# A hybrid diffusion layer on one core: modulation rows built by GpSimd inside the attention, block sums divided between the last head group and VectorE

## The chip, the core and the metric

The kernel runs on one NeuronCore of a Trainium2 chip. The metric is the device time of one execution in microseconds (us). Three runs of the kernel before took 1834.32, 1835.56 and 1839.87 us; their median is 1835.56.

Engine names: PE is TensorE (PEld its weight loads), DVE is VectorE, ACT is ScalarE, POOL is GpSimd, SP is the engine whose queue issues most DMAs.

## What is computed

One layer over 1024 latent tokens and 256 context tokens, width 1024, in float32. Cut to what matters here:

```python
mod = silu(c) @ w_mod + b_mod                  # 6 parts of 1024
sh1, sc1, g1, sh2, sc2, g2 = split(mod, 6)
hx = rmsnorm(x, norm1_g) * (1 + sc1) + sh1
q, k, v, u, B, C, ga, gc = split(hx @ w_in)    # context: k, v alone
o = windowed_attention(rope(q), rope(k), v, k_ctx, v_ctx, sink)
y = B * conv3(C * u)                           # depthwise, width 3
merged = sigmoid(ga) * (o @ w_pa) + sigmoid(gc) * (y @ w_pc)
x = x + g1 * (merged @ w_out)
hx2 = rmsnorm(x, norm2_g) * (1 + sc2) + sh2
x = x + g2 * expert_choice_moe(hx2)            # 16 experts, 128 tokens each
return rmsnorm(x, final_norm_g)
```

The modulation parts sh1 and sc1 are needed at the start. The four parts g1, sh2, sc2 and g2 (parts 2 to 5, called rows here) are needed only after the products of this document: g1, sh2 and sc2 in the output projection, g2 in the experts.

## The kernel before

Float32 products are made from two fp32r parts: a high part (a copy on ScalarE) and a low part (a subtraction on VectorE or GpSimd), and three products of them.

The stages, in order: the first modulation parts and the projection to q, k and v (0 to 240 us); the attention; the products for the convolution and the branch projections; the output projection with the router; the experts (from some 1230 us).

**Attention** (`Unit`, L571 to L651, and the loop from L693). There are 32 units, 4 groups of 4 heads by 8 blocks of 128 queries. While unit n is turned and multiplied with the values, the scores of unit n+2 are computed: PE (L605, L606), a reduction on VectorE (L608), the exponential on ScalarE (L613), then `normalise` (L617): small VectorE steps on 128x4 (L620, L622, L623) and four multiplications of the probabilities by GpSimd (L625). The transposes of a unit (L630, into two PSUM tiles named psT) need these. Between them a filler (`pour`) puts in the products of the gate blocks (L40 to L44), whose weights pass through three SBUF tiles named raw. In units 4, 10, 16 and 22 `x_sums` (L653) makes the block sums of x by ten GpSimd steps of 128x512 (L657); it uses two raw tiles. No order is written out for this part: a planner orders each engine's instructions by readiness and by their place in the program, and tile reuse gives the waits.

**Product stage** (`Pair`, the loop from L1056). From here the order of all five engines is the written one. Twenty pairs of 128-column blocks are multiplied by a scheme of seven block products (`product`, L850, 12 matmuls each on L795) instead of eight: sums of weights by VectorE (`sums13`, L826; `sums24`, L837), splits of these (`split_big`, `split22`, `split11`, ScalarE on L809 and VectorE on L810), partial sums from PSUM (L1088, L1121) and the four results (`quad`, L856). Pairs 0 to 11 give C, U and B blocks in turn (kinds 0, 1, 2), where a B pair also does the convolution (`conv`, L899) on ScalarE and VectorE (L907 to L910); pairs 12 to 15 multiply the attention output, 16 to 19 y. Their right-hand operands are block sums too: of the attention output (`o_rows`, `sums_of`, `sums_out`, L927 to L942, four sets by at_turn on L1008) and of y (four sets, L994). `op_load` and `op_split` (L950, L967) bring them in during pairs 11 and 15 and split them. `at_turn(n, slot, f)` hangs a step behind product slot `slot` of pair n.

**Rows** (`Row`, L732 to L766; L998 to L1006). In the same stage the four rows are made, one in each three pairs: eight DMAs of 128x1024 of w_mod by SP, each scaled by silu(c) on ScalarE (L743) and added up by GpSimd (L745); then a split (L751, L752), a DMA of the bias issued by GpSimd (L754), and in pairs 2, 5, 8 and 12 `total`: four matmuls with a column of ones (L760) into psT or psa tiles, two VectorE additions of the bias (L761, 1x512 each), for sc2 one more step with norm2_g (L765), and a DMA to DRAM (`rowd`). The matmuls stand ahead of slot 6:

```python
            if n in (2, 5, 8, 12) and slot == 6:
                st["row"].total([psT(), psT()] if n % 2 == 0 else [psa.tile([128, 512], F32, name=f"w{c}") for c in range(2)])
```

An odd pair takes its results in `psT(), psT(), psB(), psF()` (L848), an even one in four psa tiles; so a row's tiles are those that the pair after it takes first.

## Time and profile before

| | |
|---|---|
| median of 3 runs | 1835.56 us |
| profiled execution, its own time | 1834.67 us |
| span of its instructions | 1832.9 us |
| granted clock, mean over the span | 0.967 of full speed |
| attention, first transpose to the last | 256.3 to 583.6 us |
| gate products alone | 583.6 to 614.6 us |
| product stage | 614.6 to 1086.9 us |

The span runs from the first to the last instruction; 1.8 us lie around it. Busy time of an engine is the sum of its instructions; a row of windows gives, for a stretch, the busy time of each engine, how many instructions it ran, and the granted clock of PE as a share of 2.4 GHz. Matmuls overlap their neighbours, so their own durations are longer than their distance.

### The profile page before, as it was taken

Reading aid. Unit: us, or ns where it says so; the run is one execution under the profiler, and the core shown is the slowest. Engines: PE = TensorE matmul, PEld = TensorE weight load, DVE = VectorE, ACT = ScalarE, POOL = GpSimd, SP = SyncE. Lnnn points to the kernel's source line nnn. Section 1 sums busy time; section 2 is a strip of 40 time slices with the busy share of each in tenths; the row PEclk is TensorE's granted clock in tenths of the full one; section 3 lists DMA queues with packets and bytes.
Section 4 is the critical chain, followed back from the end, with each engine's and each line's share of the span. In section 5 each row is a group of like instructions: output and inputs, shape, how many; then the busy total and the mean of one; then the engine's idle time right before and its main releaser. Section 6 shows DMA issues by size and latency. Waiting matters only on the chain.

```text
span 1832.9 us, 24346 instructions
## 1 busy us (share of the span) xinstructions
PE 1717.3 (94%) x8421; PEld 1386.4 (76%) x8421; DVE 1462.0 (80%) x1990; ACT 1041.4 (57%) x1482; POOL 574.7 (31%) x372
## 2 busy tenths in 40 slices
PE   8999999999999989888799889959999999999997
PEld 5778878888888867667577667847888888888875
DVE  6756558788775488887987885578999999999997
ACT  5643167677775334333444343226777887877875
POOL 0000326355231145365763322241023223322101
PEclk8999999999999989898899999978999999999999
DMA  9353354243423737346657245678999999999955
GB/s 342 130 161 115 127 183 141 80 152 123 146 62 107 264 102 228 123 133 229 231 161 253 71 137 200 242 283 325 338 398 396 385 398 395 385 398 396 343 196 195
DMA packets 210861, 415.71 MB, mean 227 GB/s; under 512 B 17643, under 2 KB 107051, under 8 KB 209202
## 3 DMA queue, kind: packets, MB, share of 16 engines
q1 hardware_dynamic: 182226, 368.20, 56.1%
q0 software_dynamic: 6912, 25.51, 4.7%
q10 hardware_dynamic: 21600, 20.45, 3.2%
q8 instruction: 66, 1.08, 0.2%
q14 instruction: 57, 0.47, 0.1%
HBM read 343.31 MB, written 70.80 MB: 226 GB/s over the span
## 4 chain that ended last, share of the span: by engine, by line
PE 65%; DVE 13%; issue 4%; ACT 2%; DMA 1%; POOL 1%; POOLq 0%; ACTq 0%; DVEq 0%; SPq 0%
PE psA L1639 19%; PE w L795 5%; PE psB L1639 5%; PE psF L1639 5%; PE psA L1223 4%; PE psT L630 3%; PE psT L795 3%; PE psF L40 2%; PE psF L42 2%; PE psF L44 2%; PE psB L643 2%; PE psB L642 2%; PE psA L605 2%; PE psA L606 2%; PE psT L1624 2%
## 5 line engine op out<-in xcount | busy, mean ns | idle before, releaser
L1639 PE MATMUL psA<-part,xeh 128*128 128x512 f32 x1024 | 281.9, 392 | 0.5 <-ACT xeh L1627 0.5
L1639 PEld LDWEIGHTS psA<-part,xeh 128*128 128x128 f32 x1024 | 191.4, 188 | 40.0 <-ACT xeh L1627 1.0
L1674 POOL DMA_INDIRECT md<-ye,idxs x15 | 109.0, 7265 | 213.1 <-DVE ye L1671 213.1
L1639 PE MATMUL psA<-part,xel 128*128 128x512 f32 x512 | 163.5, 390 | 0.0
L625 POOL TENSOR_SCALAR p<-p,l 128x640 f32<-128x640 f32 (+1 forms) x128 | 100.1, 801 | 177.3 <-DVE l L623 52.6
L1497 DVE TENSOR_TENSOR part<-er,part 128x1024 fp32r<-128x1024 f32 x118 | 138.4, 1219 | 5.4 <-ACT part L1495 2.0
L1495 ACT CAST part<-er 128x1024 fp32r<-128x1024 f32 x118 | 123.7, 1057 | 32.9 <-PE psA L1639 19.9
L809 ACT CAST whi<-raw 128x1024 fp32r<-128x1024 f32 x40 | 42.0, 1050 | 172.2 <-DVE raw L840 111.0
L608 DVE CUSTOM_DVE_ANT_0 sn<-psA,msk,nsink 128x640 f32<-128x640 f32 (+1 forms) x128 | 107.4, 844 | 23.9 <-PE psA L606 13.8
L634 DVE TENSOR_TENSOR tl<-psT,th 128x512 fp32r<-128x512 f32 x152 | 104.0, 687 | 26.3 <-ACT th L633 24.9
L745 POOL TENSOR_TENSOR mp<-mp,mp 128x1024 f32<-128x1024 f32 x28 | 73.7, 2632 | 151.2 <-ACT mp L743 150.2
L633 ACT CAST th<-psT 128x512 fp32r<-128x512 f32 x152 | 88.4, 585 | 50.2 <-PE psT L630 49.3
L613 ACT ACTIVATE p<-sn,nm 128x640 f32<-128x640 f32 (+1 forms) x128 | 102.9, 805 | 21.7 <-DVE nm L608 19.6
L1639 PEld LDWEIGHTS psA<-part,xel 128*128 128x128 f32 x512 | 96.3, 188 | 20.5 <-DVE xel L1628 0.3
L1497 DVE TENSOR_TENSOR part<-mh,part 128x1024 fp32r<-128x1024 f32 x88 | 105.1, 1220 | 5.1 <-ACT part L1495 2.4
L1497 DVE TENSOR_TENSOR part<-ml,part 128x1024 fp32r<-128x1024 f32 x88 | 105.3, 1219 | 4.3 <-ACT part L1495 1.6
L1495 ACT CAST part<-ml 128x1024 fp32r<-128x1024 f32 x88 | 92.2, 1052 | 26.0 <-PE psA L1639 17.5
L1495 ACT CAST part<-mh 128x1024 fp32r<-128x1024 f32 x88 | 92.1, 1052 | 25.2 <-PE psA L1639 16.6
L1497 DVE TENSOR_TENSOR part<-mp,part 128x1024 fp32r<-128x1024 f32 x85 | 100.8, 1219 | 6.7 <-ACT part L1495 3.8
L1495 ACT CAST part<-mp 128x1024 fp32r<-128x1024 f32 x88 | 91.9, 1052 | 24.7 <-PE psA L1639 16.2
L1639 PE MATMUL psB<-part,hhh 128*128 128x512 f32 x256 | 98.6, 396 | 0.2 <-ACT hhh L1627 0.2
L810 DVE TENSOR_TENSOR wlo<-raw,whi 128x1024 fp32r<-128x1024 f32 x40 | 52.9, 1322 | 55.5 <-ACT whi L809 55.5
(506 smaller groups left out, 4730.9 us busy)
## 6 DMA issues: line engine op xcount, KB each, us to landing
raw<-in_w_in_dram SPq DMA_DIRECT2D x49, 512.0 KB, 5.6
er<-in_w_exp_down_dram SPq DMA_DIRECT2D x47, 512.0 KB, 8.8
er<-in_w_exp_up_dram SPq DMA_DIRECT2D x38, 512.0 KB, 5.6
mp<-in_w_exp_gate_dram SPq DMA_DIRECT2D x36, 512.0 KB, 6.0
mh<-in_w_exp_up_dram SPq DMA_DIRECT2D x33, 512.0 KB, 5.8
ml<-in_w_exp_up_dram SPq DMA_DIRECT2D x33, 512.0 KB, 6.2
mp<-in_w_mod_dram SPq DMA_DIRECT2D x32, 512.0 KB, 5.4
er<-in_w_exp_gate_dram SPq DMA_DIRECT2D x32, 512.0 KB, 5.5
```

What stands on the lines that cost most here:

```text
L608: nc.vector.tensor_tensor_reduce(out=sn, in0=sp[:, 512 - n:768], in1=msk.rearrange("p a b -> p (a b)")[:, mo * 128:mo * 128 + n + L], op0= ...
L613: nc.scalar.activation(out=p, in_=sn, func=AF.Exp, scale=-1.0, bias=self.nm4[:, h:h + 1], accum_out=self.l4[:, h:h + 1])
L625: nc.gpsimd.tensor_scalar(self.pr[h], self.pr[h], l4[:, h:h + 1], 1.0, op0=OP.mult, op1=OP.mult)
L633: nc.scalar.copy(out=th, in_=pt)
L634: nc.vector.tensor_tensor(out=tl, in0=pt, in1=th.bitcast(F32), op=OP.subtract)
L745: nc.gpsimd.tensor_tensor(out=self.acc, in0=self.w[k], in1=self.acc, op=OP.add)
L795: nc.tensor.matmul(ps_, lhsT=w[a][:, o + k], rhs=xs[b][:, k], start=(first and k + a + b == 0), stop=(k == 3 and a == 1), skip_group_check ...
L1223: nc.tensor.matmul(pa[:, s], lhsT=a[t // 2][k // 4][:, k % 4, ts], rhs=w[k][:, s], start=(j == 0 and a is mh and w is woh), stop=(j == NK ...
L1495: nc.scalar.copy(out=hi, in_=raw)
L1497: eng.tensor_tensor(out=lo, in0=raw, in1=hi.bitcast(F32), op=OP.subtract)
L1639: nc.tensor.matmul(outs[s], lhsT=lh[:, k], rhs=wt[:, s * 512:s * 512 + 512], start=(k == 0 and n == 0), stop=(k == NK - 1 and n == 2))
L1674: nc.gpsimd.indirect_dma_start(out=md, out_offset=bass.IndirectOffsetOnAxis(ap=idxs[:, e:e + 1], axis=0), in_=ye, in_offset=None, compute_ ...
```

## The change

Rows. The class `Row` and all its calls in the product stage are removed. `mod_row`, a generator, makes a row during the attention: w_mod is loaded into raw tiles, scaled and added by GpSimd alone, split by ScalarE and GpSimd, summed over partitions by four matmuls whose left operand is a two-column one-hot, so that the two halves of the row land in two partitions of one psT tile, and completed by VectorE on 2x512. One step of it is called in slots 1 and 4 of every unit except 4, 10, 16 and 22; a row has ten steps. Its two accumulators lie in a new pool `os`, closed at the end of the attention; the pool `tmp` of the product stage takes its place.

Block sums of the attention output: sets 0 and 1 (heads of groups 0 and 2) are made by GpSimd in units 25 to 31, in the tiles of `os`; sets 2 and 3 stay in pairs 2 and 5 and are subtracted by VectorE. Block sums of y: all four sets are subtracted by VectorE in place of GpSimd. `sums_of`, `sums_out` and `o_rows` move up in the file and take the engine or the tiles as arguments.

```diff
+    onehot = consts.tile([128, 4], FR, name="onehot")
...
+        for i in range(3):
+            nc.vector.tensor_scalar(onehot[:, i:i + 1], ones, float(i == 1), None, op0=OP.mult)
...
+    def sums_of(eng, which, ks, p11, p12, p21, p22):
+
+        for o_, a, b in ((p11, p12, p11), (p12, p22, p12), (p22, p22, p11), (p21, p21, p22)):
+            eng.tensor_tensor(out=o_, in0=a, in1=b, op=OP.subtract)
...
+    def mod_row(n):
+
+        part = n + 2
+        acc = osp.tile([128, 1024], F32, name=("o1", "o2")[n % 2])
+
+        def load(k):
+            w = raw_tile()
+            nc.sync.dma_start(out=w, in_=w_mod[k * 128:(k + 1) * 128, part * 1024:part * 1024 + 1024])
+            return w
+
+        w = load(0)
+        yield
+        for k in range(NK):
+            nc.gpsimd.tensor_scalar(w if k else acc, w, sf[:, 0, k:k + 1], 1.0, op0=OP.mult, op1=OP.mult)
+            if k:
+                nc.gpsimd.tensor_tensor(out=acc, in0=w, in1=acc, op=OP.add)
+            if k < NK - 1:
+                w = load(k + 1)
+                yield
+        small = raw_tile()
+        br, nr = small[0:2, 0:512], small[0:2, 512:1024]
+        nc.sync.dma_start(out=br, in_=b_mod[:, part * 1024:part * 1024 + 1024].rearrange("o (h f) -> (o h) f", h=2))
+        if part == 4:
+            nc.sync.dma_start(out=nr, in_=norm2_g.rearrange("o (h f) -> (o h) f", h=2))
+        hi = stage.tile([128, 1024], FR, name="raw", bufs=3)
+        lo = osp.tile([128, 1024], FR, name=("o1", "o2")[1 - n % 2])
+        nc.scalar.copy(out=hi, in_=acc)
+        nc.gpsimd.tensor_tensor(out=lo, in0=acc, in1=hi.bitcast(F32), op=OP.subtract)
+        yield
+        pf = psT()[0:2]
+        for hf in range(2):
+            cs = slice(hf * 512, hf * 512 + 512)
+            for v in (hi, lo):
+                nc.tensor.matmul(pf, lhsT=onehot[:, 1 - hf:3 - hf], rhs=v[:, cs], start=(hf == 0 and v is hi), stop=(hf == 1 and v is lo))
+        nc.vector.tensor_tensor(out=br, in0=pf, in1=br, op=OP.add)
+        if part == 4:
+            nc.vector.scalar_tensor_tensor(out=br, in0=br, scalar=1.0, in1=nr, op0=OP.add, op1=OP.mult)
+        yield
+        nc.sync.dma_start(out=rowd[n].rearrange("(h f) -> h f", h=2), in_=br)
...
+        if n in (25, 29):
+
+            o1, o2 = (osp.tile([128, 2, 512], F32, name=f"o{a}") for a in (1, 2))
+            o = o_rows((n - 25) // 4, o1.rearrange("p a b -> p (a b)"), [o2[:, 0], o2[:, 1]])
+        if n in (27, 31):
+            sums_of(nc.gpsimd, *o)
+            sums_out(*o)
...
+            if s in (1, 4) and n not in (4, 10, 16, 22):
+                next(mod_steps, None)
...
     for m in range(4):
-        at_turn(3 * m + 4, 2, lambda: sums_of(*st["ys"]))
+        at_turn(3 * m + 4, 2, lambda: sums_of(nc.vector, *st["ys"]))
...
-    for ks, b in enumerate((17, 38, 59, 68)):
-        at_turn(0, b - 5, lambda ks=ks: o_rows(ks))
-        at_turn(0, b, lambda: sums_of(*st["o"]))
+    for ks, b in ((2, 17), (3, 38)):
+        at_turn(0, b - 5, lambda ks=ks: o_late(ks))
+        at_turn(0, b, lambda: sums_of(nc.vector, *st["o"]))
...
-            if n in (2, 5, 8, 12) and slot == 6:
-                st["row"].total([psT(), psT()] if n % 2 == 0 else [psa.tile([128, 512], F32, name=f"w{c}") for c in range(2)])
```

## Rows read from the trace of the kernel before

**Rows 1.** The page, part 1: busy time of each engine over the span.

```profile
PE 1717.3 (94%) x8421; PEld 1386.4 (76%) x8421; DVE 1462.0 (80%) x1990; ACT 1041.4 (57%) x1482; POOL 574.7 (31%) x372
```

**Rows 2.** Windows by stage: from:to, length, busy of each engine, PEclk, DMA share, GB/s.

```profile
256.30:514.90 258.60, 255.72 (x1486) 217.17 (x1487) 206.47 (x436) 189.28 (x400) 120.12 (x133) 1.00 0.41 124
...
614.60:847.80 233.20, 206.52 (x853) 163.48 (x852) 182.29 (x166) 86.06 (x99) 102.83 (x48) 0.93 0.50 161
847.80:935.10 87.30, 68.09 (x257) 51.06 (x255) 77.11 (x54) 39.22 (x42) 67.05 (x29) 0.90 0.57 193
```

**Rows 3.** Windows by pair: pairs 1, 2, 3, 5, 8, 9, 10, 12 and 16.

```profile
634.00:653.40 19.40, 19.40 (x86) 15.79 (x85) 14.38 (x14) 9.52 (x11) 8.59 (x4) 1.00 0.64 192
653.40:682.70 29.30, 20.72 (x90) 15.71 (x88) 26.06 (x22) 8.72 (x10) 14.92 (x8) 0.92 0.18 53
682.70:704.70 22.00, 22.00 (x84) 17.71 (x85) 15.37 (x19) 7.99 (x9) 4.06 (x2) 0.88 0.69 221
...
724.20:754.50 30.30, 21.00 (x90) 15.76 (x88) 27.00 (x22) 8.82 (x10) 18.16 (x9) 0.92 0.31 96
...
795.80:825.60 29.80, 21.01 (x89) 15.74 (x87) 26.50 (x22) 8.82 (x10) 17.56 (x9) 0.93 0.29 93
825.60:847.80 22.20, 22.20 (x84) 17.86 (x85) 14.02 (x18) 7.99 (x9) 1.57 (x1) 0.87 0.74 260
847.80:873.50 25.70, 21.52 (x86) 16.79 (x85) 21.41 (x17) 9.40 (x11) 25.07 (x13) 0.93 0.63 200
...
893.70:935.10 41.40, 26.96 (x89) 18.59 (x87) 37.82 (x25) 18.34 (x20) 28.06 (x11) 0.84 0.39 134
...
994.20:1029.00 34.80, 25.34 (x85) 18.36 (x84) 31.42 (x22) 16.16 (x20) 23.05 (x9) 0.80 0.37 126
```

**Rows 4.** Waits from 614.6 to 847.8 us: us in total, times, longest us.

```profile
PEld psT L795 <- DVE mp L761: 14.7, 2, 7.4
...
PEld w L795 <- DVE mp L761: 7.3, 1, 7.3
```

**Rows 5.** Windows around the end of pair 2.

```profile
675.40:682.70 7.30, 0.37 (x3) 0.01 (x1) 7.26 (x6) 0.00 (x0) 5.34 (x3) 0.67 0.00 0
682.70:686.70 4.00, 4.00 (x9) 3.13 (x10) 2.78 (x4) 1.99 (x2) 0.00 (x0) 0.50 0.57 206
```

**Rows 6.** Two lines of VectorE: duration in ns, min/median/max, first and last start.

```profile
L829 DVE TENSOR_TENSOR raw<-raw x20: 675/682/2301, 595.8 to 1060.7; 128x512 f32<-128x512 f32 x20
...
L875 DVE TENSOR_TENSOR q<-w,q x16: 676/683/685, 688.0 to 1072.7; 128x512 f32<-128x512 f32 x16
```

**Rows 7.** Timeline of GpSimd and VectorE in pair 11: start us, us.

```profile
891.73 10.22 POOL L974 TENSOR_TENSOR t<-t,t 128x2048 fp32r<-128x2048 f32 x2 [3.30 <-ACT t L973]
...
889.44 1.27 DVE L908 SCALAR_TENSOR_TENSOR mp<-mp,cols,mp 128x1023 f32<-128x1023 f32 x1
...
891.95 5.58 DVE L908 SCALAR_TENSOR_TENSOR mp<-mp,cols,mp 128x1023 f32<-128x1023 f32 x1
```

**Rows 8.** Groups by shape, 614.6 to 847.8 us: busy us, mean ns.

```profile
L745 POOL TENSOR_TENSOR mp<-mp,mp 128x1024 f32<-128x1024 f32 x22 | 56.9, 2585 | 150.9 <-ACT mp L743 150.2
L930 POOL TENSOR_TENSOR mp<-mp 128x512 f32<-128x512 f32 x7 | 11.0, 1565 | 0.2
...
L810 DVE TENSOR_TENSOR x<-raw,x 128x1024 fp32r<-128x1024 f32 x9 | 11.0, 1217 | 0.0
```

**Rows 9.** GpSimd and VectorE steps of the attention: two of a timeline, three by line.

```profile
302.00 3.14 POOL L625 TENSOR_SCALAR p<-p,l 128x640 f32<-128x640 f32 x4
...
314.67 2.71 POOL L625 TENSOR_SCALAR p<-p,l 128x512 f32<-128x512 f32 x4
...
L625 POOL TENSOR_SCALAR p<-p,l x128: 689/803/1782, 255.6 to 570.7; 128x640 f32<-128x640 f32 x96, 128x512 f32<-128x512 f32 x32
...
L657 POOL TENSOR_TENSOR raw<-x,x x16: 1279/1294/2277, 178.6 to 446.0; 128x512 f32<-128x512 f32 x16
...
L620 DVE TENSOR_TENSOR es<-sink,nm x32: 150/161/1184, 252.6 to 567.6; 128x4 f32<-128x4 f32 x32
```

70 lines of the change are left out of this document (17 added, 53 removed).

## The prediction, made before the change was run

> **What bounds the kernel now.** I read the busy shares first: PE is busy 94% of the span and POOL 31% [rows 1], so a gain has to come from the places where PE stands still, and GpSimd has room somewhere. The windows by stage show where [rows 2]. In the attention (256.3 to 514.9 us) PE is busy 255.7 of 258.6 us and POOL 120.1. In pairs 0 to 9 of the product stage PE is busy 206.5 of 233.2 us, at a granted clock of 0.93, in pairs 10 to 12 only 68.1 of 87.3, while DVE is busy 182.3 and 77.1 us.
>
> The windows by pair [rows 3] give the unit of the argument. An undisturbed pair (pair 1; 0, 4, 7, 14, 15 and 17 to 19 are within 0.3 us of it) takes 19.4 us, all of it PE. Over that, pairs 2, 5 and 8 take 9.9, 10.9 and 10.4 us more and pair 3 2.6 more (6 the same) and pair 9 2.8: 39.2 us together. Pair 10 is 6.3 over, pair 12 22.0, pair 16 15.4; pairs 11 and 13 are 0.8 and 0.9 over. So 85 us of the stage are not products. The waits name the first cause [rows 4]: PE waited three times, 22 us, for VectorE's additions on L761, the last step of a modulation row, which hold a PSUM tile that the next pair wants first. The windows around the first of them show what follows [rows 5]: PE did 0.37 us of work in 7.3 us, and the next 4 us ran at a granted clock of 0.50, the lower level (1.2 GHz). That is the excess of pairs 3, 6 and 9.
>
> Why VectorE is so late there is seen in the price of one instruction [rows 6]: L829, with both inputs in SBUF, takes 0.68 us at the median and 2.30 at worst, while L875 with one input in PSUM stays between 676 and 685 ns. In the timeline [rows 7] a conv step on VectorE takes 1.27 us while GpSimd is quiet and 5.58 us beside a 128x2048 subtraction of GpSimd. So each two-input instruction of GpSimd is paid on VectorE too, when VectorE reads two SBUF operands. The Trainium skill ("SBUF — State Buffer", section "SBUF: two separate sides") calls the port pair of the two an exclusive lock, held for a whole instruction; the trace agrees in kind. By that rule each of the two such subtractions of pair 12 could hold VectorE for its whole 5.1 us and (c) below would be nearer to its lower bound; by the row one costs 4.3 us, and the sum goes by the row.
>
> **The change, part by part.**
> (a) Row work out of pairs 0 to 9. GpSimd loses 22 additions of 2.59 us there (56.9 us), 3 row splits of the same size and all 20 block-sum subtractions (such as L930's seven of 1.57 us) [rows 8]; nothing else of GpSimd's busy 102.8 us is left [rows 2]. ScalarE loses its multiplications by L743, PE the 12 row matmuls, SP its row loads, VectorE the six L761 additions. VectorE gains subtractions at the free price: 8 for two sets of block sums of y and 8 for two of the attention output, 16 x 0.68 = 10.9 us. Is VectorE fast enough then? Per pair it has seven 512-wide steps (two sums before, two after, one split, two partial sums) at 0.68 and three 1024-wide splits at 1.22 [rows 8], so 8.4 us; a finished C block costs 3 more steps, a U or B block 7 each (11.6 us per three pairs), the convolution four at 1.27, the moved sums 2.7 per set. Three pairs: 25.2 + 11.6 + 5.1 + 5.4 = 47.3 us against 58.2 us of PE. Only pairs 2 and 5 are over, 8.4 + 4.8 + 5.1 + 2.7 = 21.0 against 19.4; the 1.6 us run into a pair with 13 us of work. I leave 3 us of the 39.2 and take a gain of 36. Bounds: 25 (only the three waits of 7.3 us and the 12 matmuls go, VectorE stays late) and 39.
> (b) Pair 10. GpSimd was busy 25.1 of its 25.7 us, all of it row additions and block sums, all gone. VectorE gets one y set (2.7) in a pair that then needs about 16. Taken: 5.5 of 6.3; bounds 0 and 6.3.
> (c) Pair 12. The two 128x2048 subtractions of the operand split stay on GpSimd, and with them VectorE's two slow conv steps [rows 7]. What goes: one row addition in the queue ahead of them (2.6), the row split between them and the next operand split (2.6), the bias row's DMA (0.5 of GpSimd's time) and the last four row matmuls (0.9): 6.6, and VectorE enters the pair less late. Taken 8 of 22; bounds 0 and 18. The y sums of pair 13, now on VectorE, wait there for the late multiplications and the DMA that stores y; behind them stand a split and two sums that PE needs half a pair later, so I cost them at nothing; without that cover they cost their 2.7.
> (d) Pair 16: two operand splits collide with no row near. No change.
> (e) What the attention pays. Sixteen row matmuls come in; at 19.4/84 = 0.23 us each 3.7 us, and PE has no idle time to put them in. Four times one of two transpose tiles is held for a VectorE addition; I add 2.3 for that. ScalarE's four copies and SP's 32 loads lie beside it, as do the one-hot's three tiny steps. The GpSimd work must fit: a 128x640 multiplication is 0.785 and a 128x512 one 0.68 [rows 9], so 128x1024 is 0.785 + 3 x 0.107 = 1.11 (estimate); an addition is 2.59. Per row 8 x 1.11 + 8 x 2.59 = 29.6, four rows 118.4; with the 120.1 of before 238.5 of 258.6 us: 92% busy. Per unit it is 2 x 3.7 + 3.1 for the softmax scaling (L625), 10.5 against a unit of 258.6/25 = 10.3; it fits only because four units carry none, and because this stretch isn't held to the written order: the first block sums of x, written in unit 4, ran at 178.6 us [rows 9], so steps can move ahead to where GpSimd idles. VectorE's softmax steps on L620 have two SBUF inputs and can be blocked (161 ns at the median, 1184 at worst); VectorE has 52 us free in this stretch. SP's loads rotate over three shared raw tiles; a late addition holds a load, and the queries of the next unit stand behind it. Taken: 6 us; bounds 3.7 (nothing is removed here, so no gain) and 40.
> The two attention-output sums on GpSimd in the last group (8 x 1.29 = 10.3 us) stand where no row steps are left: nothing. Their tiles must be free before the first product's copy at about 617 us, 30 us after the last unit: nothing.
>
> Sum: 36 + 5.5 + 8 - 6 = 43.5 us. The profiled execution took 1834.67 us, 0.9 below the median of the runs; 1834.7 - 43.5 = 1791.2, against the median 1792. About 0.3% (5.5 us) is what a measurement of this kernel can tell from no change.
>
> **Rivals.**
> R1, GpSimd saturates. If VectorE's blocks stretch its work by the fifth that L930 shows (1.57 against 1.29 us [rows 8, 9]), 238.5 becomes 286, 28 us over the stretch: the attention pays 28 instead of 6, and the time is 1834.7 - 49.5 + 28 = 1813. For: 92% is close to full. Against: L657 keeps 1294 ns at the median in this very stretch, where VectorE mostly reads PSUM. The Trainium skill ("GPSIMD Engine Reference", section "4.1 Engine selection") speaks for this one: it sends elementwise work on a tile to VectorE, since two-input work is about twice as slow on GpSimd. The rows agree (1294 against 682 ns).
> R2, slower than before. GpSimd runs its queue in order; if row steps stand ahead of each unit's scaling, the transposes behind it become the bound of every unit. At 1.11 + 2.59 twice and the scaling at up to 1.78 each (its worst), a unit would take 14.5 us. It decides from 12.3 us per unit on, where 25 units give back 50. At 12.6 the attention pays 58: 1834.7 - 49.5 + 58 = 1843. Against: PE stood still for only 2.9 us of this stretch [rows 2], with three of the four block sums of x (ten steps of 1.29 us each) already in the same queue.
> R3, VectorE stays the bound. The added subtractions land in the conv pairs, the waits of L761 go but the lateness stays: (a) falls to 25, (b) and (c) to 2 each, 23 in all: 1835 - 23 = 1812. For: VectorE was busy 26.1 of 29.3 us in pair 2. Against: most of that was blocking.
> R4, the planner puts the rows elsewhere: ahead of the attention, where GpSimd idles, with PE free of them. Then (e) is 4 and (c) may reach 15: 1782.
>
> **How the numbers follow.** My forecast holds 0.45, R4 0.14, R1 0.18, R3 0.12, R2 0.08; 0.03 is for a draw of gain and cost. Faster is 0.89, same 0.03, slower 0.08. From the bounds, all gains full and (e) at 4 give 1835 - 39 - 6 - 14 + 4 = 1780, with pair 16 helped by a lighter queue 1776; R1 and R3 end at 1812 to 1813; with 35 of (e)'s 40 the time is 1820. The range is 1776 to 1820.
>
> **What would show it.** Right: pairs 2 to 9 at 19.4 to 20 us with the clock at 1.00; L829, L839 and L840 near 0.68 there and POOL near zero; pair 12 near 33, pair 16 near 35; in the attention POOL above 85% and PE still above 97%. Wrong: transposes (L630) waiting for L625, or row matmuls waiting for GpSimd's row split; pairs 2 and 5 still above 24 us; SP's queue waiting for raw tiles.

## The result, and the profile after

The changed kernel takes 1850.49 us (median of 5 runs, 1842.41 to 1854.85) beside 1835.56: a ratio of 1.0077 with the interval [1.0057, 1.0096], so slower by 0.8%, where 1792 was forecast. Its profiled execution took 1854.85 us, 20.2 more than that of before; it is the longest of the five, so the lengths read from it below are, all together, some 4 us above those of the median run. The page's first part, of the kernel after:

```profile
PE 1728.0 (93%) x8421; PEld 1393.8 (75%) x8421; DVE 1432.0 (77%) x2012; ACT 1008.6 (54%) x1450; POOL 546.7 (30%) x376
```

It hardly differs from [rows 1]; the stages do. Windows by stage of the kernel after (attention, pairs 0 to 11), columns as in [rows 2]:

```profile
257.40:655.50 398.10, 349.58 (x1898) 290.30 (x1896) 286.20 (x540) 239.35 (x500) 263.87 (x232) 0.92 0.44 138
...
686.50:920.70 234.20, 233.95 (x1010) 189.12 (x1008) 167.37 (x212) 70.90 (x86) 7.57 (x4) 1.00 0.37 121
```

And the whole attention of the kernel before, first transpose to last:

```profile
256.30:583.60 327.30, 324.43 (x1883) 275.55 (x1883) 255.46 (x536) 235.12 (x495) 138.56 (x157) 1.00 0.37 110
```

The attention grew by 70.8 us (398.1 - 327.3). In it PE stood still for 48.5 us instead of 2.9 (+45.6), and was busy for 25.2 more, at a granted clock of 0.92 instead of 1.00. GpSimd's busy time rose by 125.3 us. The product stage shrank from 472.3 to 421.1 us (686.5 to 1107.6). Windows by pair of the kernel after, pairs 2, 3, 5, 10, 12 and 16:

```profile
725.40:744.80 19.40, 19.40 (x85) 15.77 (x84) 17.29 (x21) 6.51 (x8) 0.00 (x0) 1.00 0.33 108
744.80:764.70 19.90, 19.77 (x85) 15.61 (x84) 15.23 (x22) 5.12 (x7) 0.00 (x0) 1.00 0.32 107
...
784.20:803.60 19.40, 19.40 (x86) 15.76 (x85) 17.31 (x21) 6.49 (x8) 0.00 (x0) 1.00 0.34 109
...
881.80:901.20 19.40, 19.40 (x85) 15.78 (x84) 12.63 (x17) 5.19 (x8) 0.00 (x0) 1.00 0.34 108
...
920.70:956.60 35.90, 25.21 (x85) 17.60 (x84) 33.02 (x20) 17.39 (x19) 23.60 (x8) 0.86 0.38 134
...
1015.20:1049.50 34.30, 26.14 (x85) 18.78 (x84) 30.95 (x21) 16.23 (x20) 23.03 (x9) 0.80 0.37 130
```

Beside [rows 3] pairs 2 and 5 fall from 29.3 and 30.3 us to 19.4, pair 10 from 25.7, pair 12 from 41.4 to 35.9. So the stage gained what was forecast, and the attention took it all back and 20 us more.

**Where PE stood still in the attention.** Windows of 10 us of the kernel after:

```profile
277.00:287.00 10.00, 4.02 (x27) 3.43 (x25) 3.26 (x7) 1.63 (x4) 10.00 (x10) 0.89 0.16 39
287.00:297.00 10.00, 3.15 (x9) 2.76 (x10) 4.46 (x3) 3.63 (x7) 9.92 (x8) 0.50 0.15 41
...
387.00:397.00 10.00, 10.00 (x58) 8.61 (x58) 6.43 (x15) 5.71 (x13) 0.63 (x1) 0.99 0.10 28
...
447.00:457.00 10.00, 5.34 (x30) 4.15 (x28) 8.95 (x8) 2.65 (x8) 10.00 (x9) 0.92 0.22 76
457.00:467.00 10.00, 4.58 (x13) 3.50 (x14) 8.24 (x7) 1.42 (x3) 8.04 (x8) 0.50 0.04 7
```

GpSimd (the fifth engine column) is busy for 10 of 10 us where PE (the first) has 3 to 5, and for 0.63 where PE is full. Its mean of 66% (263.9 of 398.1) hides full stretches and empty ones. After PE has stood still the clock is at 0.50, its lower level of 1.2 GHz: each stop is paid a second time.

The full stretches have a plain reason. The program calls two row steps in nearly every unit, but GpSimd doesn't run two in each. Timeline of GpSimd, kernel after (L628 scales the probabilities of a unit, L713 and L715 are a row step, L660 is a block sum of x):

```profile
345.43 2.70 POOL L628 TENSOR_SCALAR p<-p,l 128x512 f32<-128x512 f32 x4
348.10 2.40 POOL L715 TENSOR_TENSOR o<-raw,o 128x1024 f32<-128x1024 f32 x1
350.48 1.12 POOL L713 TENSOR_SCALAR raw<-raw,sf 128x1024 f32<-128x1024 f32 x1
...
362.31 3.47 POOL L660 TENSOR_TENSOR raw<-x,x 128x512 f32<-128x512 f32 x2
365.77 3.11 POOL L628 TENSOR_SCALAR p<-p,l 128x640 f32<-128x640 f32 x4
...
381.42 6.22 POOL L628 TENSOR_SCALAR p<-p,l 128x640 f32<-128x640 f32 x8
```

Between two scalings, from 348.1 to 365.8 us, stand four multiplications and four additions of a row and two block sums, 17.6 us; at 381.4 the scalings of two units follow each other with nothing between.

The waits of the attention, kernel after (us in total, times, longest):

```profile
PE psB L645 <- ACT th L636: 27.4, 6, 12.8
...
ACT whi L212 <- DMA raw<-in_w_in_dram: 18.2, 7, 7.4
...
ACT es L624 <- DVE es L623: 15.7, 6, 6.0
...
ACT whi L677 <- POOL raw L660: 12.8, 1, 12.8
...
PE psF L40 <- ACT gs L336: 7.9, 3, 7.0
...
PE psT L633 <- POOL p L628: 5.7, 9, 2.4
```

PE hardly waits for GpSimd itself (last line). It waits for ScalarE, and ScalarE for something late. The timeline of the longest stop, 12.8 us, kernel after:

```profile
278.06 0.57 ACT L636 CAST th<-psT 128x512 fp32r<-128x512 f32 x1
...
278.49 3.74 POOL L660 TENSOR_TENSOR raw<-x,x 128x512 f32<-128x512 f32 x3
...
290.18 1.25 POOL L660 TENSOR_TENSOR raw<-raw,x 128x512 f32<-128x512 f32 x1
...
291.46 1.04 ACT L677 CAST whi<-raw 128x1024 fp32r<-128x1024 f32 x1 [12.83 <-POOL raw L660]
...
293.24 0.56 ACT L636 CAST th<-psT 128x512 fp32r<-128x512 f32 x1
...
293.85 0.80 PE L645 MATMUL psB<-th,v2t 128*128 128x512 f32 x1 [12.84 <-ACT th L636]
```

The block sums of x (L660), first made at 178.6 us before [rows 9], now begin at 278.5, behind row steps (without rows they begin at 182.3); ScalarE's next instruction in order is the copy of their result (L677), and the copy of the transposed probabilities (L636), which has long been ready and which PE wants, stands behind it. The second stop (7.0 us from 432.0) has the same shape one step further off: the gate weights' load (L211) waited in SP's queue for a raw tile that GpSimd's addition (L715) still held, ScalarE's split of these weights (L212) waited for the load, and the copy for the gate products (L336) stood behind it. Timeline of ScalarE and PE, kernel after:

```profile
437.45 1.04 ACT L212 CAST whi<-raw 128x1024 fp32r<-128x1024 f32 x1 [7.43 <-DMA raw<-in_w_in_dram]
438.40 0.58 ACT L336 COPY gs<-psF 128x512 f32<-128x512 f32 x1
...
439.03 0.79 PE L40 MATMUL psF<-x,whi 128*128 128x512 f32 x1 [7.04 <-ACT gs L336]
```

The third and fourth (5.0 and 5.1 us from 452.3 and 458.1) come from two of VectorE's small additions (L623, L625), which took 6.34 and 5.49 us: ScalarE's exponential (L624) waits for the first, and the copy L636 stands behind it; the subtraction L637 stands behind the second on VectorE's own queue. Timeline of VectorE, GpSimd, ScalarE and PE, kernel after:

```profile
449.60 0.69 DVE L637 TENSOR_TENSOR tl<-psT,th 128x512 fp32r<-128x512 f32 x1
...
450.20 6.34 DVE L623 TENSOR_TENSOR es<-sink,nm 128x4 f32<-128x4 f32 x1
450.32 1.29 POOL L660 TENSOR_TENSOR raw<-raw 128x512 f32<-128x512 f32 x1
...
451.58 1.27 POOL L660 TENSOR_TENSOR raw<-x,x 128x512 f32<-128x512 f32 x1
...
452.81 1.26 POOL L660 TENSOR_TENSOR raw<-x,raw 128x512 f32<-128x512 f32 x1
454.03 1.26 POOL L660 TENSOR_TENSOR raw<-raw 128x512 f32<-128x512 f32 x1
455.25 1.26 POOL L660 TENSOR_TENSOR raw<-raw,x 128x512 f32<-128x512 f32 x1
456.49 1.11 POOL L713 TENSOR_SCALAR raw<-raw,sf 128x1024 f32<-128x1024 f32 x1
456.57 0.20 ACT L624 ACTIVATE es<-es 128x4 f32<-128x4 f32 x1 [5.98 <-DVE es L623]
456.69 0.57 ACT L636 CAST th<-psT 128x512 fp32r<-128x512 f32 x1
456.88 5.49 DVE L625 TENSOR_TENSOR l<-l,es 128x4 f32<-128x4 f32 x1 [0.34 <-ACT es L624]
...
457.31 0.80 PE L645 MATMUL psB<-th,v2t 128*128 128x512 f32 x1 [4.96 <-ACT th L636]
457.57 1.27 POOL L660 TENSOR_TENSOR raw<-x,raw 128x512 f32<-128x512 f32 x1
458.80 2.33 POOL L715 TENSOR_TENSOR o<-raw,o 128x1024 f32<-128x1024 f32 x1
461.09 1.26 POOL L660 TENSOR_TENSOR raw<-raw,x 128x512 f32<-128x512 f32 x1
...
463.22 0.79 PE L646 MATMUL psB<-tl,v2t 128*128 128x512 f32 x1 [5.11 <-DVE tl L637]
```

These four stops are 29.9 of the 48.5 us.

### The profile page after: what moved, and what is told of

It is laid out like the page before. It is cut to its first block, busy times and chain, and to the rows that moved or that the text cites. A ratio compares the mean times of both kernels' runs of the same rounds, so it can differ in the third digit from the quotient of the medians.

```text
span 1853.1 us, 24278 instructions
## 1 busy us (share of the span) xinstructions
PE 1728.0 (93%) x8421; PEld 1393.8 (75%) x8421; DVE 1432.0 (77%) x2012; ACT 1008.6 (54%) x1450; POOL 546.7 (30%) x376
## 4 chain that ended last, share of the span: by engine, by line
PE 75%; DVE 8%; POOL 7%; issue 4%; DMA 3%; ACT 2%; SPq 0%; POOLq 0%; ACTq 0%; DVEq 0%
PE psA L1650 19%; PE w L835 7%; PE psB L1650 5%; PE psF L1650 5%; PE psT L835 5%; PE psA L1234 4%; PE psA L400 3%; PE psA L398 2%; PE psA L399 2%; PE psT L633 2%; PE psF L835 2%; PE psF L40 2%; PE psF L42 2%; PE psF L44 2%; POOL p L628 2%
## 5 line engine op out<-in xcount | busy, mean ns | idle before, releaser
L1506 ACT CAST part<-er 128x1024 fp32r<-128x1024 f32 x118 | 123.7, 1056 | 32.9 <-PE psA L1650 19.9
L637 DVE TENSOR_TENSOR tl<-psT,th 128x512 fp32r<-128x512 f32 x152 | 103.8, 686 | 36.4 <-ACT th L636 35.3
L611 DVE CUSTOM_DVE_ANT_0 sn<-psA,msk,nsink 128x640 f32<-128x640 f32 (+1 forms) x128 | 107.2, 842 | 31.8 <-PE psA L609 17.6
L628 POOL TENSOR_SCALAR p<-p,l 128x640 f32<-128x640 f32 (+1 forms) x128 | 102.0, 818 | 87.0 <-PE psB L645 30.2
L636 ACT CAST th<-psT 128x512 fp32r<-128x512 f32 x152 | 88.6, 584 | 62.6 <-PE psT L633 61.4
L919 POOL TENSOR_TENSOR mp<-q,mp 128x512 f32<-128x512 f32 x15 | 24.4, 1653 | 293.8 <-DVE q L913 280.1
L1506 ACT CAST part<-mh 128x1024 fp32r<-128x1024 f32 x88 | 92.2, 1053 | 25.2 <-PE psA L1650 16.5
L1506 ACT CAST part<-mp 128x1024 fp32r<-128x1024 f32 x88 | 92.0, 1053 | 24.5 <-PE psA L1650 16.0
L633 PE MATMUL psT<-identr,p 128*128 128x128 f32 x608 | 98.8, 281 | 6.0 <-POOL p L628 5.7
L633 PEld LDWEIGHTS psT<-identr,p 128*128 128x128 f32 x608 | 78.9, 144 | 29.7 <-POOL p L628 9.5
```

What stands on the lines that cost most here:

```text
L611: nc.vector.tensor_tensor_reduce(out=sn, in0=sp[:, 512 - n:768], in1=msk.rearrange("p a b -> p (a b)")[:, mo * 128:mo * 128 + n + L], op0= ...
L628: nc.gpsimd.tensor_scalar(self.pr[h], self.pr[h], l4[:, h:h + 1], 1.0, op0=OP.mult, op1=OP.mult)
L633: nc.tensor.transpose(pt[:, h * 128:(h + 1) * 128], self.pr[h][:, ci * 128:(ci + 1) * 128], ident)
L636: nc.scalar.copy(out=th, in_=pt)
L637: nc.vector.tensor_tensor(out=tl, in0=pt, in1=th.bitcast(F32), op=OP.subtract)
L1506: nc.scalar.copy(out=hi, in_=raw)
```

## The experiments

Each kernel's time is a median beside the kernel before of the same chip (1834 to 1837 us). "Attention" is the length from the first transpose to the last (before 327.3, after 398.1), "products" that of the product stage (472.3, 421.1); both are read from the profiled execution, while "less" and "more" go by the medians of the times. The five runs of the change lie between 1842 and 1855 us, so a difference of 7 or 8 us from it is near what they can tell from nothing. Edits are against the changed kernel unless another is named.

**No rows at all.**

```diff
         for n in range(4):
-            yield from mod_row(n)
+            small = raw_tile()[0:1]
+            nc.sync.dma_start(out=small, in_=b_mod[:, (n + 2) * 1024:(n + 3) * 1024])
+            yield
+            nc.sync.dma_start(out=rowd[n:n + 1], in_=small)
+            yield
```

> The changed kernel without the making of the rows in the attention: each row is the bias alone (no loads of w_mod, no multiplications, additions, split or row matmuls); everything else stands. In the changed kernel the stretch from the first transpose to the first product lasts 429 us against 358 before, and the product stage 421 against 472. Theory A (the rows are the whole of the attention's loss, and nothing of the product stage hangs on them): the stretch is back to 355 to 360 us, the product stage stays at 421, and the time is 1850 - 71 = 1779, 1770 to 1785. Theory B (the block sums of the attention output on GpSimd in the last group, or another planned order, carry a part): the stretch stays above 370 us and the time above 1792.

1783.70 us (0.9717 [0.9701, 0.9733]): attention 327.2, products 421.1. This is Theory A: the attention's loss is the row work and nothing else; the block sums of the last head group cost nothing there.

**No rows, and the other block sums back on GpSimd** (against the kernel without rows):

```diff
-        at_turn(3 * m + 4, 2, lambda: sums_of(nc.vector, *st["ys"]))
+        at_turn(3 * m + 4, 2, lambda: sums_of(nc.gpsimd, *st["ys"]))
...
-        at_turn(0, b, lambda: sums_of(nc.vector, *st["o"]))
+        at_turn(0, b, lambda: sums_of(nc.gpsimd, *st["o"]))
```

> As the run without rows (each row is the bias alone), but the block sums of y and the two late ones of the attention output are subtracted by GpSimd as before the change. It parts the 51 us that the product stage gained. Theory P (row additions, row splits and row sums were the whole of it): the product stage stays at 421 to 425 us, time 1782 to 1788. Theory S (the block sums' move to VectorE carries a part, since each of them on GpSimd holds VectorE): 428 to 445 us, time 1790 to 1806.

1782.98 us (0.9713 [0.9697, 0.9729]), products 420.4. Moving these block sums to VectorE is worth nothing by itself: once the rows are gone, GpSimd's block sums disturb nobody.

**One load for each row in place of eight** (the other products are of the same block):

```diff
-            nc.gpsimd.tensor_scalar(w if k else acc, w, sf[:, 0, k:k + 1], ...)
+            nc.gpsimd.tensor_scalar(tmpw if k else acc, w, sf[:, 0, k:k + 1], ...)
...
-                w = load(k + 1)
                 yield
```

> Each row loads one block of w_mod in place of eight and uses it eight times; GpSimd's multiplications and additions stay as many and as long. So the three raw tiles turn 28 times less, and SP's queue no longer waits for GpSimd's additions (116 us of SP waiting on L707, L721 and L211 for them in the changed kernel). Seven eighths of w_mod are left out of the rows. Theory R (the shared raw tiles and SP's queue behind them cause the stalls): the stretch falls from 429 to about 365 to 380 us, and the time to 1785 to 1800. Theory L (GpSimd's instructions as such, by holding up VectorE and by standing ahead of work that ScalarE's queue waits for): the stretch stays above 405 us and the time above 1825.

1842.74 us (1.0036 [1.0017, 1.0054]), attention 381.4: 8 us less than the change, so Theory L's time. None of the four stops is left, and in their place PE waits for GpSimd's scaling, 24.6 us where it was 5.7:

```profile
PE psT L633 <- POOL p L628: 24.6, 21, 9.0
```

**The small additions on ScalarE** (L623, L625):

```diff
-            nc.vector.tensor_tensor(out=es, in0=sink[...], in1=self.nm4, op=OP.add)
-            nc.scalar.activation(out=es, in_=es, func=AF.Exp)
-            nc.vector.tensor_tensor(out=l4, in0=l4, in1=es, op=OP.add)
+            for h in range(4):
+                nc.scalar.activation(out=es[:, h:h + 1], in_=self.nm4[:, h:h + 1], func=AF.Exp, bias=sink[:, c:c + 1])
+            for h in range(4):
+                nc.scalar.activation(out=l4[:, h:h + 1], in_=l4[:, h:h + 1], func=AF.Identity, bias=es[:, h:h + 1])
```

> The two small additions of the softmax denominator (L623, L625, 128x4, two SBUF inputs on VectorE) are made by ScalarE instead, in eight steps of about 0.19 us per unit; the rows stay as in the changed kernel. VectorE's waits behind GpSimd on these two lines (39 us busy in the attention against 10 at their free price, so 29 us) are gone; ScalarE gets 1.3 us more per unit, 42 us in all, in a stretch where it is busy 60%. Theory L2 (VectorE's small additions starved by GpSimd are the main stall): the stretch falls by 15 to 30 us, time 1820 to 1835. Theory R or T: within 10 us of the changed kernel, 1842 to 1858.

1843.86 us (1.0045 [1.0029, 1.0061]), attention 389.8: 7 us less, within what Theories R and T gave. Again the wait for the scaling takes over (24.5 us).

**The row steps later in the unit**, in slots 3 and 4:

```diff
-            if s in (1, 4) and n not in (4, 10, 16, 22):
+            if s in (3, 4) and n not in (4, 10, 16, 22):
```

> The row steps of a unit are called in slots 3 and 4, behind the softmax scaling of the unit after next, in place of slots 1 and 4. Nothing is left out; GpSimd's instructions are the same ones. The runs so far took away the loads (8 us back), the two-input additions (27 us) and VectorE's small additions (7 us), each alone, of 67 us that the rows cost; what is left is that GpSimd's queue is in order and the row steps stand ahead of the scaling, so that transposes wait (PE on L628: 5.7 us in the changed kernel, 25 us without the loads). Theory T (the order on GpSimd's queue): the stretch from first transpose to first product falls from 429 to 400 us or less, time under 1825. Theory L (VectorE is held up by GpSimd whatever the order, and ScalarE's queue waits behind both): within 10 us of the changed kernel, 1840 to 1858.

1853.63 us (1.01 [1.008, 1.012]), attention 396.5: no gain. But the edit hardly moved anything: the order of this part is the planner's, and as in the change four multiplications and four additions of a row and two block sums stand between the same two scalings (344.0 to 361.7 us here). So Theory T is not tested by this run.

**Each addition replaced by two multiplications** of one input:

```diff
-                nc.gpsimd.tensor_tensor(out=acc, in0=w, in1=acc, op=OP.add)
+                nc.gpsimd.tensor_scalar(w, w, sf[:, 0, k:k + 1], 1.0, op0=OP.mult, op1=OP.mult)
+                nc.gpsimd.tensor_scalar(w, w, sf[:, 0, k:k + 1], 1.0, op0=OP.mult, op1=OP.mult)
```

> Each addition of a row (two SBUF inputs, 2.39 us) is replaced by two more multiplications (one SBUF input, 1.13 us each), so GpSimd is busy nearly as long and loads and tiles turn as before, but 28 two-input instructions are gone. The sum over the blocks is left out. Theory L2 (two-input instructions of GpSimd lock VectorE's two-input steps out): the long L623 and L625 (6.3 and 5.5 us in the changed kernel) fall under 1.5 us, and the stretch falls by 25 us or more, to 400 or less; time below 1825. Theory R and theory T (GpSimd merely late): the stretch stays at 420 to 430 us, the time at 1842 to 1855.

1823.43 us (0.9941 [0.9925, 0.9958]), attention 358.3: 27 us less, for nearly the same length of work (2 x 1.13 against 2.39 us by the medians); that is Theory L2's time. Its first sign did not come: L623 and L625 still took up to 4.45 and 3.05 us, each beside block sums of x. And more than the form changed: the first block sums of x began at 229.7 us, ahead of the attention, and not at 278.5. So the 27 us are not shown to be the form's alone.

**The additions left out.**

```diff
-            if k:
-                nc.gpsimd.tensor_tensor(out=acc, in0=w, in1=acc, op=OP.add)
```

> The changed kernel without the 28 additions of the rows (67 us of GpSimd's time), multiplications, loads, splits and row matmuls kept. With multiplications in the additions' place the time was 1823. Theory Q (GpSimd's total in the attention decides): well below that, 1785 to 1800, stretch 365 to 380. Theory L2 (the two-input instruction as such is what costs): no better than 1823 by more than 8 us, 1815 to 1828.

1803.77 us (0.9826 [0.9806, 0.9846]), attention 346.7, between the two theories. Of the rows' 67 us 47 go with the additions; the 32 multiplications, the splits and the loads keep 20. Here too the first block sums of x come ahead of the attention (216.0 us), so the 47 are not the additions' own length alone.

**The block sums of x left out**, so that ScalarE's and VectorE's split reads a block of x itself:

```diff
-        sub(t1, part(0, 0, 1), part(0, 0, 0))
...
-            rv = r[n].rearrange("p (a b) -> p a b", a=2)
+            rv = part(0, n, 1)[:, None, :].to_broadcast([128, 2, 512])
```

> As the run without the block sums of x, but their splits read x directly, so no raw tile is taken (in that run two ScalarE copies waited 28 us for raw tiles that row additions held, a stall of the experiment's own making). Rows as in the changed kernel; the block sums of x are left out. Theory Q (row steps and block sums of x bunch on GpSimd's queue, and VectorE, ScalarE and PE wait behind the bunch): the stretch from first transpose to first product, 429 us in the changed kernel and 358 without rows, falls to 375 or less; time 1803 or less. Theory L (the row work costs by itself, at any density): 395 us or more, time 1820 or more.

1832.34 us (0.9988 [0.9977, 0.9998]), attention 373.2: 18 us less, so Theory L's side. The first stop is gone, but ScalarE now waits 26.9 us for the row accumulator, at the row's own split (waits of this kernel, below). A first form of this, whose stand-in copies on ScalarE waited for GpSimd too, gave 1833.60 us.

```profile
ACT raw L714 <- POOL o L703: 26.9, 4, 11.1
```

**The block sums of x in the projections**, row steps in all 32 units:

```diff
-        if n in (4, 10, 16, 22):
-            x_sums((n - 4) // 6)
...
+        if n in (2, 4, 6, 8):
+            x_sums(n // 2 - 1)
```

> The changed kernel with the four block sums of x called in the loop of the projections (after pairs 2, 4, 6 and 8 of token blocks), so that the rows have GpSimd's spare time in the attention to themselves, two steps in every unit. Nothing is left out. Theory Q: attention 330 to 345 us, projections 0 to 10 us longer, time 1788 to 1810. Theory L: attention 370 us or more, or the projections 25 us longer as with the rows there; time 1822 or more.

1866.98 us (1.0182 [1.0165, 1.0199]): the worst. The first transpose comes at 291.5 us instead of 257.4 and the attention still takes 375.7. The row steps still stand in bunches, with no block sum among them: from 482.5 to 498.7 us five multiplications and four additions lie between two scalings.

**The rows in the projections**, GpSimd as in the change:

```diff
+    def mod_row(n):
...
+        if n > 0:
+            for _ in range(5):
+                next(mod_steps, None)
...
-            if s in (1, 4) and n not in (4, 10, 16, 22):
-                next(mod_steps, None)
```

> The rows are made by GpSimd alone as in the change, but called in the loop of the projections to q, k and v, five steps per pair of token blocks, where GpSimd is busy 23 of 135 us before. The accumulator is one tile; the low part of a row goes into a raw tile, the bias into gs tiles. Nothing is left out. Theory T (the cost in the attention comes from work there that waits on GpSimd's queue, and the projections have none): projections and attention grow by 0 to 15 us, product stage 421, time 1785 to 1800. Theory L (GpSimd's two-input steps hold VectorE up wherever VectorE reads two SBUF operands, as the rotary sums and splits of the projections do; and the first loads of the attention stand on GpSimd's queue): growth of 25 us or more, time 1810 or more.

1845.99 us (1.0051 [1.0035, 1.0068]). The attention is clean (328.5), but begins at 319.1 us: 62 us lost ahead of it, with ScalarE waiting for GpSimd's accumulator in the same way (up to 14.0 us at a time). So the rows on GpSimd cost about as much in another stage: the price isn't peculiar to the attention.

**The rows by GpSimd in the product stage again**, but with the two-column matmuls and one PSUM tile that the next pair doesn't want first, and the block sums as in the change:

```diff
...
+            if n in (2, 5, 8, 12) and slot == 6:
+                st["row"].total(psB() if n % 2 == 0 else psa.tile([128, 512], F32, name="w2"))
```

> The rows go back to the product stage (multiplied by ScalarE, added by GpSimd, as before the change), but the four row matmuls use the two-column one-hot and one PSUM tile, the one that the next pair fills only in its slot 5 (psB or w2) in place of two that it fills first. Block sums as in the changed kernel. Nothing is left out. Theory W (before, the stall at a row's end was the PSUM tile, and VectorE has room once the block sums no longer lock it out): attention 327 us as before, product stage 423 to 440, time 1786 to 1803. Theory V (28 additions and 4 splits on GpSimd hold VectorE up as much as before, and PE waits for partial sums and splits): product stage 450 or more, time 1813 or more.

1821.92 us (0.9926 [0.991, 0.9943]), products 461.7: 10 us better than before, and 40 us from the stage without rows.

**Two rows by GpSimd, one step a unit**; the other two are the bias alone:

```diff
...
-            if s in (1, 4) and n not in (4, 10, 16, 22):
+            if s == 4 and n not in (4, 10, 16, 22):
```

> Rows 0 and 2 are made by GpSimd as in the change, one step in each unit (slot 4 only); rows 1 and 3 are left out (bias alone). Half the row work, no unit with two steps. Theory C (capacity: a unit is 10.3 us, scaling 3.1, one step 3.7, so one step fits and two hardly): the attention loses under 10 us, time 1784 to 1794. Theory L (each step costs by itself, wherever there is room): half of the 67 us, time 1812 to 1822.

1820.45 us (0.9904 [0.9888, 0.9921]): 36.7 over the kernel without rows, where all four rows cost 66.8: nearly in proportion, which is Theory L's time. Theory C is not refuted by it, since its condition, one step in a unit, was not met: from 465.7 to 487.6 us four multiplications and four additions of a row and five block sums stand between two scalings.

**The rows by VectorE in the attention**, loads and places as in the change:

```diff
-            nc.gpsimd.tensor_scalar(w if k else acc, w, sf[:, 0, k:k + 1], ...)
-            if k:
-                nc.gpsimd.tensor_tensor(out=acc, in0=w, in1=acc, op=OP.add)
+            if k:
+                nc.vector.scalar_tensor_tensor(out=acc, in0=w, scalar=sf[:, 0, k:k + 1], in1=acc, op0=OP.mult, op1=OP.add)
+            else:
+                nc.scalar.activation(out=acc, in_=w, func=AF.Copy, scale=sf[:, 0, k:k + 1])
...
-        nc.gpsimd.tensor_tensor(out=lo, in0=acc, in1=hi.bitcast(F32), op=OP.subtract)
+        nc.vector.tensor_tensor(out=lo, in0=acc, in1=hi.bitcast(F32), op=OP.subtract)
```

> The rows stay in the attention, in the same slots and with the same loads, but VectorE makes them (one fused multiply and add of 128x1024 for each block of w_mod, about 1.2 us by L810 of the kernel before, and the low part) and ScalarE the first multiplication of each row; GpSimd keeps no row instruction. Theory L (what costs is the row work on GpSimd's queue): 28 x 1.2 + 4 x 1.2 = 38 us of VectorE work beside some 52 us that it has free, so the attention loses little: last transpose near 590, time 1783 to 1800, faster than the version with VectorE's rows in the product stage (1802.8). Theory S (any added step costs, because each engine's in-order queue is planned tightly and the raw tiles are shared): the attention still loses 30 us or more, time above 1812.

1807.28 us (0.9836 [0.9819, 0.9852]), attention 350.7. Between the two theories: 43 us of the loss go when the rows leave GpSimd, and 24 stay on VectorE, whose step is shorter (1.28 us for what takes GpSimd 1.13 and 2.39).

**The rows by VectorE in the product stage** (against the version with GpSimd's rows there):

```diff
-            nc.scalar.activation(out=self.w[k], in_=self.w[k], func=AF.Copy, scale=sf[:, 0, k:k + 1])
             if k:
-                nc.gpsimd.tensor_tensor(out=self.acc, in0=self.w[k], in1=self.acc, op=OP.add)
+                nc.vector.scalar_tensor_tensor(out=self.acc, in0=self.w[k], scalar=sf[:, 0, k:k + 1], in1=self.acc, op0=OP.mult, op1=OP.add)
             else:
+                nc.scalar.activation(out=self.w[k], in_=self.w[k], func=AF.Copy, scale=sf[:, 0, k:k + 1])
...
-            nc.gpsimd.tensor_tensor(out=self.halves[1], in0=self.acc, in1=self.halves[0].bitcast(F32), op=OP.subtract)
+            nc.vector.tensor_tensor(out=self.halves[1], in0=self.acc, in1=self.halves[0].bitcast(F32), op=OP.subtract)
```

> As the run with the rows back in the product stage and one PSUM tile, but a row's block is multiplied and added in one VectorE instruction (1.22 to 1.28 us by the conv steps) in place of a ScalarE multiplication and a GpSimd addition, and the low part is made by VectorE. GpSimd has nothing to do in pairs 0 to 9. Nothing is left out. VectorE needs, per three pairs, 41.9 us + 9 x 1.25 of rows + 5.4 of block sums = 58.6 us against 58.2 of PE in the first two periods, 55.9 in the others. Theory V (GpSimd's two-input steps are what makes VectorE late, its own work fits): product stage 423 to 435 us, time 1786 to 1798. Theory F (VectorE is simply full): 440 us or more, time 1803 or more.

1802.84 us (0.9817 [0.9801, 0.9834]), products 442.2: 21 us for all four rows, half of what GpSimd's cost there. The stage's length is on the side of Theory F: VectorE's own work doesn't fit for nothing.

**The same, with the block sums of pairs 2 to 13 on GpSimd:** the edit of the second experiment.

> The same with the block sums of y and of the late attention output on GpSimd: VectorE 53.2 us per three pairs, GpSimd 5 to 10. Without rows these sums on GpSimd cost nothing (1783.0 against 1783.7). Theory F (VectorE's own load decides): 3 to 10 us faster than the run before in this list. Theory V (every GpSimd step is paid on VectorE once VectorE is nearly full): 3 to 10 us slower than it.

1806.76 us (0.9838 [0.9822, 0.9855]), products 448.8: pairs 4, 7 and 10 go from 19.4 to some 23.5, while pairs 3, 6 and 9, which have less on VectorE then, fall from some 24 to 21 or 22. So the block sums on GpSimd cost nothing without the rows; beside rows on VectorE the six sets cost 6.6 us of the stage together.

**VectorE's rows packed into two pairs of three, and sums moved to emptier pairs** (against the version with VectorE's rows in the product stage; the two late sums of the attention output go to GpSimd):

```diff
-        at_turn(3 * m + 4, 2, lambda: sums_of(nc.vector, *st["ys"]))
+        at_turn(*((3 * m + 3, 5) if m < 3 else (13, 2)), lambda: sums_of(nc.vector, *st["ys"]))
...
-        for k, (a, b) in enumerate(((0, 2), (1, 3), (2, 4), (5, 7), (6, 8), (9, 11), (10, 12), (13, 15))):
+        for k, (a, b) in enumerate(((0, 2), (1, 3), (2, 4), (5, 7), (6, 8), (7, 9), (8, 10), (9, 11))):
...
-        at_turn(*((3 * r + 2, 2) if r < 3 else (11, 6)), lambda: st["row"].split())
+        at_turn(3 * r, 13, lambda: st["row"].split())
...
-        at_turn(0, b, lambda: sums_of(nc.vector, *st["o"]))
+        at_turn(0, b, lambda: sums_of(nc.gpsimd, *st["o"]))
```

> The rows on VectorE in the product stage, its load evened out: a row's eight steps and its split end in the second of its three pairs (so not in the convolution's pair), the block sums of y come in the first pair of three, the two late sums of the attention output go back to GpSimd. By the free prices VectorE has 19.6, 17.9 and 18.3 us of work in the three pairs against 19.4 of PE. Nothing is left out. Theory E (with VectorE's rows the stalls left in pairs 3, 6 and 9, 4.5 us each, come from the convolution's pair being overfull): these fall under 1.5 us each, product stage 428 to 434 us, time 1788 to 1795. Theory F (VectorE is full over the three pairs, and evening out only moves the stall): 439 us or more, 1800 or more.

1807.50 us (0.9856 [0.9839, 0.9872]), products 449.0: no help, so Theory F.

**VectorE's rows, and the operand splits and late multiplications on VectorE too** (against the same version):

```diff
-        parts = ((nc.vector, slice(0, 2)), (nc.gpsimd, slice(2, 4)))
-        if which == 0 and j < 2:
-            parts = ((nc.gpsimd, slice(0, 4)),)
+        parts = ((nc.vector, slice(0, 2)), (nc.vector, slice(2, 4)))
...
-            nc.gpsimd.tensor_tensor(out=o_, in0=p, in1=o_, op=OP.mult)
+            nc.vector.tensor_tensor(out=o_, in0=p, in1=o_, op=OP.mult)
```

> The version with VectorE's rows in the product stage, and GpSimd's share of the operand splits (pairs 12 and 16) and the four late multiplications given to VectorE as well, so that GpSimd has no two-input instruction left in these pairs. Theory V (a two-input GpSimd instruction is paid on VectorE; what is left of pairs 12 and 16 over 19.4 us is that): VectorE gains some 9 half-splits of 1.22 us and 4 multiplications of 0.68 but loses some 15 us of blocking in pair 12, so pair 12 falls from 40.1 to below 32 us and pair 16 from 35.1 to below 30; time 1782 to 1796. Theory W (VectorE is full there by its own work): pairs 12 and 16 stay within 3 us, time 1800 to 1806.

1791.05 us (0.9764 [0.9745, 0.9783]), the best version that makes the whole layer. Pair 12 falls from 40.1 to 33.9 and pair 16 from 35.1 to 31.3: the direction of Theory V and its time, but smaller steps than it gave. The conv step that took 5.58 us beside GpSimd's subtraction [rows 7] now takes 1.28 us, in the timeline of this kernel:

```profile
863.47 1.28 DVE L935 SCALAR_TENSOR_TENSOR mp<-mp,cols,mp 128x1023 f32<-128x1023 f32 x1
864.79 1.28 DVE L937 SCALAR_TENSOR_TENSOR mp<-mp,cols,mp 128x1023 f32<-128x1023 f32 x1
```

In what is left of pair 12 PE waits for the splits themselves, ScalarE's copies as well as VectorE's subtractions.

## Why the prediction was wrong

**Steps (a) to (d) held.** (a) Pairs 0 to 9 went from 233.2 to 195.3 us, 37.9 less where 36 was taken, at a clock of 1.00, with no pair above 19.9. VectorE's moved subtractions cost nothing, as costed, and pairs 2 and 5 carry 17.3 us of VectorE work, less than the 21.0 forecast. (b) Pair 10 gave 6.3 for 5.5. (c) Pair 12 gave 5.5 for 8; that GpSimd's subtractions, which stayed, are paid on VectorE is seen in the last experiment, at a price of 6.2 us (40.1 to 33.9) and not of most of the pair's excess. (d) Pair 16 moved by 0.5. Together 51.2 us were gained where 49.5 stood in the sum; that it fits so well is in part two misses that offset each other, (a) by 1.9 and (c) by 2.5.

**Step (e) failed**: 6 us taken, upper bound 40, measured 71 (67 by the medians with and without rows). Its amounts were right: GpSimd's 1.11 and 2.59 us measured 1.13 and 2.39, and of the 125 us that it gained in the stretch 10 are block sums, so 115 were rows where 118.4 was reckoned. What failed is the overlap: how these became time. Three sentences of the step did it.

"The GpSimd work must fit" set the sum of busy times against the length of the stretch. That asks whether an engine has the time in total; PE asks at each unit whether its operand is there. PE was busy 324.4 of 327.3 us before, so it had no reserve to make up a delay with, and a stop that outlasts the lead of the pipeline stays in the end time. The sum per unit, 2 x 3.7 + 3.1, took it that each unit has its two steps. The trace shows up to 19 us of row steps and block sums between two scalings (from 443.1 to 462.4 us) and none between others; before, the most was six block sums, 8.7 us of work, and PE stood still for 2.9 us in the whole attention. No experiment spread the steps evenly, so whether four rows would fit that way is open: the price of 66.8 us for four rows and 36.7 for two is that of rows in bunches.

"Steps can move ahead to where GpSimd idles" was the wrong way round: the block sums of x moved back behind the row steps, from 178.6 to 278.5 us. Row steps come at the rate of loads through three shared raw tiles, and in GpSimd's full stretches nothing could move.

"ScalarE's four copies and SP's 32 loads lie beside it" counted their busy time, which is small, and left out their place in a queue. A copy that waits for GpSimd blocks every instruction behind it on ScalarE: this is what the trace shows at 278 to 294 us, and at 432 and 450 us for a load and for a small addition. The step named one such chain, the queries behind a held load, and put no price of its own on it. The experiments that removed one of the three (loads 8, small additions 7, block sums of x 18 us) got 33 us if they are added up, and each found the next wait, for the scaling or for the row's own split, in its place.

**The rivals.** R2's time, 1843, is the nearest, and its sign is right: 58 us were its price for the attention. Its place is not: the transposes waited for the scaling for only 5.7 us of PE's time, and only after another stop was taken away did this wait come forward (24.6 us). So the nearness of its number is in part luck. R1 fell as put, with GpSimd at 66% in the mean, though full for stretches of 20 to 40 us; R3 fell with pairs 2 and 5 at 19.4 us, R4 because nearly all of the row work stayed in the attention (ahead of it the rows lost 62 us, not 4). Together I gave the right sign 0.08: one mechanism was priced where any of four queues could carry the delay. The range, 1776 to 1820, held neither R2's time nor the last 5 us of the step's own bound of 40.

**The clock** had no term in (e). PE's 25.2 us more of busy time hold 16 row matmuls (3.7 us by the prediction's 0.23) and, for the rest, matmuls that ran longer at the lower clock after a stop, as in the windows at 0.50: some 21 us that no list of waits shows.

**What stays open.** How the 67 us divide among lateness by length, blocking of VectorE, and clock is known only by single removals, which don't add up, since the planner's order changed with them. Not tried were an order that holds the row steps to one or two in each unit, the copies behind GpSimd's results (L677, L726) put later in ScalarE's queue, and loads into tiles that gate weights don't share.

## What to carry to other kernels

Where the engine that sets the end has no idle time, work that moves beside it is not free because another engine has room in total: ask of each result of the slower engine which instruction consumes it, on which in-order queue, and what the bound engine wants from behind it. Price it as a share of its length and not as nothing. Against the attention without rows, added work here cost 0.61 us per us (70.9 us for 115.5 on GpSimd; by the rows below, 23.5 for 38.8 on VectorE), 0.68 with two rows (34.6 for 51.0) and 0.37 with multiplications alone (31.1 for 84.2); it is a share of this kernel and its order, not a constant. Look at the order in which the work will run, not the one in which it is written, and look at busy time in stretches as short as the lead of the pipeline, not over the stage. Where the same work can be one fused instruction on the faster engine, that is the first thing to try: it cut the rows from 67 to 24 us in the attention and from 40 to 21 in the product stage.

The windows of the attention, first of the kernel without rows, then of the one with the rows on VectorE (VectorE's is the third engine column):

```profile
254.40:581.60 327.20, 324.44 (x1881) 275.83 (x1882) 256.45 (x536) 235.32 (x495) 148.33 (x165) 1.00 0.41 123
```

```profile
255.80:606.50 350.70, 336.32 (x1896) 281.50 (x1895) 295.22 (x567) 240.83 (x501) 169.17 (x175) 0.98 0.50 157
```

## What the hardware showed that was not expected

A VectorE addition of 128x4 elements took 6.34 us (median 0.16). It began at 450.20 us, while GpSimd was in a block sum, and ended at 456.54, after five more of these had run back to back, each begun after VectorE's own start. The Trainium skill ("SBUF — State Buffer", section "SBUF: two separate sides") calls the shared pair of ports an exclusive lock that goes to whichever starts first for its whole instruction. The trace agrees that such a VectorE instruction is held completely, but one instruction of GpSimd would be 1.3 us here; it was held through five, and the measurement decides. It ended as a one-input multiplication began (456.49). The next addition (L625) began beside that multiplication and was held all the same, for 5.49 us, through three two-input instructions, until GpSimd stood still at 462.35. Without rows on GpSimd no addition of L623 took over 1.25 us, though the block sums of x ran there too; why is open. VectorE's subtraction with an operand in PSUM kept its 0.69 us in the same stretch (L637 at 449.60).

Whether the form of an instruction counts beside its length is not shown. Two one-input multiplications in place of one two-input addition, for 0.13 us less of GpSimd's time each, gave back 27 us, but the order of the block sums changed with them.
